# Mixer, latent stores and embedding projection: other engines and queues, one more buffer each

## The chip, the cores and the metric

One Trainium2 chip, one core of it. The metric is the device time of one execution of the whole program, in microseconds (us). The program is one inference step of one layer; all inputs and weights lie in the chip's memory at the start, and the outputs lie there at the end.

## What is computed

1024 prompt rows and 8 x 16 sample rows of width 2048 are treated as one set of 1152 tokens. The reference, cut to what matters here:

```python
xn = rms_norm(x, norm_g)
u, g_pool, c_q, c_kv, k_r, g_mla = split(xn @ w_in)            # 1024, 1024, 512, 256, 64, 1024 columns
pool_out = multiscale_pool(pool_hist, u, pos0, w_pool, pool_scale) * silu(g_pool)
new_pool = concatenate([pool_hist, u], axis=1)[:, -15:]
q, k, v  = ...                                                 # from c_q, c_kv and the caches
mla_out  = chunk_causal_attention(q, k, v) * silu(g_mla)
h = x + concatenate([pool_out, mla_out], axis=-1) @ w_out
y = h + sigmoid(rms_norm(h, ple_norm_g) @ w_ple_gate + b_ple_gate) * (p @ w_ple)

def multiscale_pool(...):      # 4 groups of 256 channels, windows 2, 4, 8, 16
    d = mean of the last w rows of u - u                       # over 15 rows of history and the row itself
    return (d @ w_pool[group]) * pool_scale
```

`p` is a 256-wide input per token; `p @ w_ple` is the embedding projection. For the samples the 15 rows of history come from the input `state_pool`, for the prompt they are zero.

## The kernel before

Everything is held transposed: 128 channels on the partitions, tokens along the row, in three blocks of 384 tokens (`TB`); block 2 is the last 256 prompt tokens and the 128 sample tokens. An f32 product is made as three matmuls over operands split in a high and a low part: ScalarE writes the high part (L68), VectorE (in some places GpSimd) the difference (L69), and `mm3` issues the three matmuls (L77 to L79).

The stages, by the time of the trace: sums of `x` and of the first weights (to about 150 us); the input projection `x @ w_in` in two halves of its inner dimension, "chunk 0" (to 400) and "chunk 1" (to 803); latents to keys and queries, with block 0 of the embedding projection beside (to 980); the first half of its block 1, alone (to 1000); the samples' attention, with the rest of block 1 inside (to 1250); embedding block 2 (to 1285); the prompt's attention and the output projection with its gate (to the end).

**The projection** saves multiplications by taking weights in sums and differences. `Quick.sums` (L150) loads two raw weights `r0`, `r1` (tile `wraw`, three buffers), writes the sums `w12` into a tile `wt` (one buffer, called `a` in the code) and the sums `w34` over `r0`, and splits each into `wh`, `wl`. In chunk 1 the result of each product is added to the partial result of chunk 0, loaded as `q` (L512, three buffers), and handed to `finish` (L521). It scales block 2 if need be, takes SiLU for gates, and stores the result `o` (three buffers) to a scratch tensor by L535: `u` and `gp` (mixer input and its gate), `gm` (attention's gate), `cq`, `ckv`. These 90 stores are on SyncE's queue (SP in the profile), in between the loads of `q` and of the weights.

**The mixer** (`Pool`) runs over chunk 1's products from about 505 to 760 us, on TensorE's spare bank `aux`. For group `g` and token block `t`, `fetch` loads 128 channels of `u` back from scratch (L704; with 15 columns of history of the block before, L703), `gates` loads the two gate tiles into `ev` (L710), `tile` forms the window sums by doubling on VectorE (`window`, L689) and the difference `d` (L693), `split` splits `d` into `dh`, `dl`, and `mix` multiplies by the group's weights `pwh`, `pwl` into `aux`, scales by the gate on VectorE (L749) and stores `mixp` (L750). Loads of `u` and gates are on GpSimd's queue (POOL). In block 2 `tile` also stores the new history (L727), loads the samples' history `us` (L729, one buffer, SP's queue), copies the samples' tokens behind it (L730), sums it, and stores the samples' new history (L732).

**The embedding** (`Embed.block`) takes for each of 16 column tiles a weight `wraw` (L786, ScalarE's queue), splits it, multiplies into `p` (two banks) or `k` (a bank lent by the attention), copies the result to `ev` (two buffers, VectorE, L794) and stores it to the scratch `ple` (L795, ScalarE's queue).

**Order.** The code is written in one order and a scheduler, which lays all instructions on a simulated time line, decides the order on each engine. Each engine then runs its own list strictly in that order, and so does each queue: a DMA whose data are not ready holds all that stand behind it on its engine. Tiles come from rings: a tile's next user waits until all readers of the one that many allocations back are done.

Of the kernel before, what the change touches and what calls it, by code (L numbers as in the profile page):

```python
# [8 lines left out]
AF = mybir.ActivationFunctionType  # L9
ALU = mybir.AluOpType  # L10
# [6 lines left out]
NB = 8  # L17
NS = 16
NTOK = SEQ + NB * NS
P = 128  # L20
KT = D // P
TB = 384
# [108 lines left out]
class Quick:  # L131
# [19 lines left out]
    def sums(self, src, c, rest):  # L151

        k, nc = self.k, self.k.nc
        sub = nc.vector.tensor_tensor
        r0, r1 = [self.raw(s, c) for s in src]
        w0 = self.hl(r0)
        a = k.t(self.tp, [P, 8, P], "wt")
        sub(a[:, :4], r1[:, :4], r0[:, :4], ALU.subtract)
        sub(a[:, 4:], r1[:, 4:], a[:, :4], ALU.subtract)
        w12 = self.hl(a)  # L160
        sub(r0[:, :4], r1[:, 4:], r1[:, :4], ALU.subtract)
        sub(r0[:, 4:], r0[:, 4:], a[:, 4:], ALU.subtract)
        w34 = self.hl(r0)
        w1 = self.hl(r1, 0 if rest else 4)
        return {1: (w0, 0), 2: (w0, 4), 5: (w12, 0), 6: (w12, 4), 7: (w34, 0), 4: (w34, 4), 3: (w1, 4),
                "rest": ((w0, 0), (w1, 0))}
# [86 lines left out]
def phase1(k, sc):  # L253
# [268 lines left out]
    def finish(i, t, ps, q):  # L522
        kind, n = kinds[i] if i < KR else ("kr", 0)
        o = o_tile()
        if q is not None:
            nc.vector.tensor_tensor(o[:], ps, q[:], ALU.add)
            ps = o[:]
        if t == 2:
            nc.vector.tensor_tensor(o[:], ps, R2[:], ALU.mult)
        if kind == "kr":  # L530
            k.later(rope_key(k, lp, aux_bank, o, kc, ks, t, sc))
            return
        if kind in ("gp", "gm"):
            nc.scalar.activation(o[:], o[:], AF.Silu)
        nc.sync.dma_start(sc[kind][t][:, n, :], o[:])  # L535
        if kind not in ("ckv", "cq"):
            return
        if (kind, t) not in acc:
            acc[kind, t] = [k.t(lp, [P, TB], f"acc{t}"), 2 if kind == "ckv" else 4]
            nc.scalar.activation(acc[kind, t][0][:], o[:], AF.Square)  # L540
        else:
            sq = k.t(lp, [P, TB], "sq")
            nc.scalar.activation(sq[:], o[:], AF.Square)
            nc.vector.tensor_tensor(acc[kind, t][0][:], acc[kind, t][0][:], sq[:], ALU.add)
        acc[kind, t][1] -= 1
        if not acc[kind, t][1]:
            k.later(latent_factor(kind, t, acc[kind, t][0]))
# [114 lines left out]
class Pool:  # L662


    def __init__(self, k, pp, aux_bank, inv, sc, wp):
        self.k, self.pp, self.aux, self.inv, self.sc = k, pp, aux_bank, inv, sc
        self.wp, self.hl, self.d = wp, [None, None], [None, None]
        self.u, self.gate = {}, {}

    def weights(self, g):  # L670
        k, pp = self.k, self.pp
# [24 lines left out]
    def fetch(self, ct, t):  # L696

        k, nc, src = self.k, self.k.nc, self.sc["u"]
        u = self.u[ct, t] = k.t(self.pp, [P, HIST + TB], "u", bufs=2)
        if t == 0:  # L700
            nc.vector.memset(u[:, :HIST], 0.0)
        else:
            nc.gpsimd.dma_start(u[:, :HIST], src[t - 1][:, ct, TB - HIST:])  # L703
        nc.gpsimd.dma_start(u[:, HIST:], src[t][:, ct, :])  # L704

    def gates(self, g, t):
        k = self.k
        for n in (2 * g, 2 * g + 1):
            self.gate[n, t] = k.t(self.pp, [P, TB], "ev", bufs=2)
            k.nc.gpsimd.dma_start(self.gate[n, t][:], self.sc["gp"][t][:, n, :])  # L710

    def tile(self, ct, t):
        k, pp, nc, io = self.k, self.pp, self.k.nc, self.k.io
        g, c2 = divmod(ct, 2)
        w = 2 << g
        d = self.d[c2] = k.t(pp, [P, TB], f"d{c2}")
        n = TB if t < NT - 1 else SEQ - TB * (NT - 1)
        u = self.u.pop((ct, t))
        s = self.window(u[:, :HIST + n], n, d[:, :n], w)
        if t == 0:  # L720

            m = w - 1
            x = k.t(pp, [P, 16], "head")
            nc.vector.tensor_tensor(x[:, :m], s[:, HIST:HIST + m], self.inv[:, :m], ALU.mult)
            nc.vector.tensor_tensor(d[:, :m], x[:, :m], u[:, HIST:HIST + m], ALU.subtract)
        if t == NT - 1:
            nc.sync.dma_start(io["npool"][ct][:, 0, :], u[:, n:n + HIST])  # L727
            us = k.t(pp, [P, NB, HIST + NS], "us")
            nc.sync.dma_start(us[:, :, :HIST], io["state_pool"][ct])  # L729
            nc.vector.tensor_copy(us[:, :, HIST:], u[:, HIST + n:].rearrange("p (b s) -> p b s", b=NB))  # L730
            self.window(us[:], NS, d[:, n:].rearrange("p (b s) -> p b s", b=NB), w, (NB,))
            nc.sync.dma_start(io["npool"][ct][:, 1:, :], us[:, :, NS:])  # L732

    def split(self):
        for c, d in enumerate(self.d):
# [3 lines left out]
    def mix(self, g, t):  # L739
        k, pp, nc, sc = self.k, self.pp, self.k.nc, self.sc  # L740
        hl = self.hl
        for o in range(2):
            n = 2 * g + o
            gate = self.gate.pop((n, t))
            ps = self.aux()
            sl = slice(o * P, (o + 1) * P)
            for c in range(2):
                k.mm3(ps[:, :TB], self.wh[:, c, sl], self.wl[:, c, sl], hl[c][0][:], hl[c][1][:], c == 0, c == 1)
            nc.vector.scalar_tensor_tensor(gate[:], ps[:, :TB], k.pool_scale[:, n:n + 1], gate[:], ALU.mult, ALU.mult)  # L749
            nc.sync.dma_start(sc["mixp"][t][:, n, :], gate[:])  # L750


def consts(k):
# [11 lines left out]
class Embed:  # L765
# [8 lines left out]
    def block(self, t, cts=range(KT), bank=None):  # L774
        k, nc, io, pl = self.k, self.k.nc, self.k.io, self.pl
        if t != self.at:
            self.at = t
            self.ph = k.t(pl, [P, 2, TB], "h", F32R)
            self.pl_ = k.t(pl, [P, 2, TB], "l", F32R)
            for c in range(2):  # L780
                raw = k.t(pl, [P, TB], "raw")
                nc.scalar.dma_start(raw[:], io["pT"][t][:, c, :])
                k.split(self.ph[:, c, :], self.pl_[:, c, :], raw[:])
        for ct in cts:
            raw = k.t(pl, [P, 2, P], "wraw", bufs=4)
            nc.scalar.dma_start(raw[:], io["w_ple"][ct])  # L786
            wh = k.t(pl, [P, 2, P], "wh", F32R, bufs=self.bufs)
            wl = k.t(pl, [P, 2, P], "wl", F32R, bufs=self.bufs)
            k.split(wh[:], wl[:], raw[:])
            ps = bank() if bank and ct % 3 else k.t(self.pp, [P, 512], "p", bufs=self.banks)  # L790
            for c in range(2):
                k.mm3(ps[:, :TB], wh[:, c, :], wl[:, c, :], self.ph[:, c, :], self.pl_[:, c, :], c == 0, c == 1)
            ev = k.t(pl, [P, TB], "ev", bufs=2)
            nc.vector.tensor_copy(ev[:], ps[:, :TB])  # L794
            nc.scalar.dma_start(self.sc["ple"][t][:, ct, :], ev[:])  # L795


class Shared:
# [881 lines left out]
```

## Time and profile before

| | |
|---|---|
| runs | 2310.47, 2302.0, 2307.72 us; median 2307.72 us |
| profiled execution | 2295.69 us, of which span 2293.9 us; mean granted TensorE clock 0.983 |
| VectorE, ScalarE, GpSimd busy | 1450.2 us (63%), 985.4 us (43%), 345.7 us (15%) |
| SyncE's queue and ScalarE's queue | 304.18 MB in 234240 packets, 23.21 MB in 19296 packets |
| GpSimd's queue | 9.56 MB in 3584 packets |

The page gives busy times of one execution over its span. `PE` is TensorE, `DVE` VectorE, `ACT` ScalarE, `POOL` GpSimd, `SP` SyncE, which only issues DMAs; "SPq" marks a DMA issue on that queue. A row of the list of waits reads "engine, tile and line that waited <- engine, tile and line (or DMA) waited for: us in all, times, longest". A row of the timeline is start, duration, engine, line, operation, out<-in, shape, and in brackets the idle time ahead of it with what ended it. The clock is the one granted to TensorE: 0.50 means that the matmuls were fed at half speed.

### The profile page before, as it was taken

To read this page: it belongs to the slowest core of one execution; us is meant where nothing else is said; L and a number is where in the kernel's file an instruction comes from. 1 tells how busy PE (TensorE), PEld (TensorE's weight loads), DVE (VectorE), ACT (ScalarE), POOL (GpSimd) and SP (SyncE) were. 2 spreads that over 40 slices of the span, in tenths; PEclk is the share of its full clock that TensorE was granted. 3 is DMA by queue.
4 is the path that set the end of the run, shared out by engine and by line. 5 is a ranking of instruction groups with operands and counts; after the bars stand their busy time and mean duration, and the time that the engine had idled before them with its cause. 6 is when DMAs were issued, how large, how long until landed. Compare 5 with 4: busy or idle time off the path is not lost.

```text
span 2293.9 us, 35989 instructions
## 1 busy us (share of the span) xinstructions
PE 2217.6 (97%) x12856; PEld 2160.4 (94%) x12856; DVE 1450.2 (63%) x3056; ACT 985.4 (43%) x2181; POOL 345.7 (15%) x317
## 2 busy tenths in 40 slices
PE   8989999999899999989999899999999999999999
PEld 7989999999899989979998799999999999999998
DVE  6787777776777668868887765555553345344343
ACT  6533335443333466756665543343342233232222
POOL 0000000001111000033552532221002221111110
PEclk9999999999999999999999799999999999999999
DMA  9574336556666766482222844443263333223221
GB/s 297 185 245 156 126 122 217 166 164 178 184 186 186 220 201 189 122 252 95 92 71 73 246 152 153 129 154 124 82 198 112 101 120 110 86 92 98 85 87 64
DMA packets 257299, 339.24 MB, mean 148 GB/s; under 512 B 45024, under 2 KB 207200, under 8 KB 257120
## 3 DMA queue, kind: packets, MB, share of 16 engines
q1 hardware_dynamic: 234240, 304.18, 42.9%
q10 hardware_dynamic: 19296, 23.21, 3.1%
q0 software_dynamic: 3584, 9.56, 1.7%
q8 instruction: 101, 1.65, 0.3%
q14 instruction: 78, 0.64, 0.1%
HBM read 235.74 MB, written 101.12 MB: 147 GB/s over the span
## 4 chain that ended last, share of the span: by engine, by line
PE 54%; DMA 7%; DVE 6%; issue 2%; ACT 2%; POOL 1%; SPq 0%; ACTq 0%; DVEq 0%; POOLq 0%
PE mm L77 8%; PE mm L79 8%; PE mm L78 8%; PE f L77 3%; PE f L79 3%; PE f L78 3%; PE k L78 2%; PE k L79 2%; PE k L77 2%; PE t L1213 1%; DMA rawcq<-cq 1%; PE o L79 1%; PE o L78 1%; PE s L78 1%; PE s L79 1%
## 5 line engine op out<-in xcount | busy, mean ns | idle before, releaser
L68 ACT ACTIVATE wh<-wraw 128x1024 fp32r<-128x1024 f32 (+3 forms) x237 | 182.2, 770 | 212.9 <-PE mm L177 125.7
L69 DVE TENSOR_TENSOR wl<-wraw,wh 128x1024 fp32r<-128x1024 f32 (+3 forms) x235 | 210.6, 897 | 69.9 <-ACT wh L68 67.3
L1536 DVE TENSOR_TENSOR ev<-mm,R 128x384 f32<-128x384 f32 x48 | 26.7, 557 | 174.2 <-PE mm L79 170.3
L1537 ACT ACTIVATE ev<-ev,gains 128x384 f32<-128x384 f32 x48 | 29.4, 612 | 224.5 <-DVE ev L1536 124.5
L71 ACT ACTIVATE wh<-wraw,gains 128x128 fp32r<-128x128 f32 x256 | 82.0, 391 | 52.5 <-ACT wh L71 31.6
L704 POOL DMA_DIRECT2D u<-u x24 | 13.1, 544 | 602.1 <-DVE frs3a L88 509.3
L1214 ACT ACTIVATE pth<-t 128x512 fp32r<-128x512 f32 (+2 forms) x96 | 46.3, 486 | 131.8 <-PE t L1213 130.8
L72 DVE SCALAR_TENSOR_TENSOR wl<-wraw,gains,wh 128x128 fp32r<-128x128 f32 x256 | 88.0, 390 | 17.5 <-ACT wh L71 16.4
L77 PE MATMUL k<-wkh,ch 128*128 128x448 f32 x256 | 95.2, 373 | 2.1 <-ACT ch L68 1.3
L78 PE MATMUL k<-wkh,cl 128*128 128x448 f32 x256 | 93.6, 365 | 0.6 <-DVE cl L69 0.6
L79 PE MATMUL k<-wkl,ch 128*128 128x448 f32 x256 | 93.7, 366 | 0.0
L79 PE MATMUL mm<-A2l,wh 128*128 128x384 f32 x256 | 86.0, 336 | 0.0
L77 PE MATMUL mm<-A2h,wh 128*128 128x384 f32 x256 | 86.0, 336 | 0.0
L78 PE MATMUL mm<-A2h,wl 128*128 128x384 f32 x256 | 86.0, 336 | 0.0
L77 PE MATMUL mm<-A0h,wh 128*128 128x384 f32 x256 | 85.8, 335 | 0.0
L79 PE MATMUL mm<-A0l,wh 128*128 128x384 f32 x256 | 85.7, 335 | 0.0
L78 PE MATMUL mm<-A1h,wl 128*128 128x384 f32 x256 | 85.7, 335 | 0.0
L78 PE MATMUL mm<-A0h,wl 128*128 128x384 f32 x256 | 85.7, 335 | 0.0
L79 PE MATMUL mm<-A1l,wh 128*128 128x384 f32 x256 | 85.5, 334 | 0.0
L77 PE MATMUL mm<-A1h,wh 128*128 128x384 f32 x256 | 85.5, 334 | 0.0
L1498 DVE TENSOR_TENSOR ev<-mm,ev 128x384 f32<-128x384 f32 x48 | 26.8, 558 | 86.3 <-PE mm L79 85.9
L1342 ACT ACTIVATE sq<-k 128x896 f32<-128x896 f32 x64 | 58.5, 914 | 51.7 <-PE k L1339 50.0
(803 smaller groups left out, 7822.6 us busy)
## 6 DMA issues: line engine op xcount, KB each, us to landing
wraw<-w_in SPq DMA_DIRECT2D x89, 512.0 KB, 4.6
part<-o SPq DMA_DIRECT2D x93, 192.0 KB, 2.7
q<-part SPq DMA_DIRECT2D x93, 192.0 KB, 3.4
wraw<-w_out SPq DMA_DIRECT2D x64, 256.0 KB, 3.4
wraw<-w_ple_gate SPq DMA_DIRECT2D x64, 256.0 KB, 3.2
ple<-ev ACTq DMA_DIRECT2D x48, 192.0 KB, 3.0
fev<-xT SPq DMA_DIRECT2D x48, 192.0 KB, 2.4
hp<-fev SPq DMA_DIRECT2D x48, 192.0 KB, 1.9
```

Source lines behind the costliest of these rows:

```text
L68: nc.scalar.activation(hi, src, AF.Copy)
L69: eng.tensor_tensor(lo, src, hi, ALU.subtract)
L71: nc.scalar.activation(hi, src, AF.Copy, scale=scale)
L72: eng.scalar_tensor_tensor(lo, src, scale, hi, ALU.mult, ALU.subtract)
L77: mm(out, sh, mh, start=start, stop=False)
L78: mm(out, sl, mh, start=False, stop=False)
L79: self.last = mm(out, sh, ml, start=False, stop=stop)
L1214: nc.scalar.activation(pth[:, :n, qq], tp[:, :n, :], AF.Copy)
L1342: nc.scalar.activation(sq[:].rearrange("p (g c) -> p g c", g=2), ps[:, :2, :KW], AF.Square)
L1498: nc.vector.tensor_tensor(h[:], ps[:, :TB], h[:], ALU.add)
L1536: nc.vector.tensor_tensor(g[:], ps[:, :TB], R[t][:], ALU.mult)
L1537: nc.scalar.activation(g[:], g[:], AF.Sigmoid, bias=k.b_ple_gate[:, ct:ct + 1])
```

## The change

Four things: the last weight sums are written into `wt` (`a`) and not over `r0`; the stores of `finish`, of `mixp` and of the new history go from SP's queue to GpSimd's; the mixer's loads of `u` and gates go the other way, and the samples' history is loaded in `fetch`, together with its `u`, into two buffers; the embedding's results are copied by ScalarE into three buffers (which the raw input shares) and stored by GpSimd's queue.

```diff
--- before.py
+++ after.py
@@ -158,9 +158,9 @@
         sub(a[:, :4], r1[:, :4], r0[:, :4], ALU.subtract)
         sub(a[:, 4:], r1[:, 4:], a[:, :4], ALU.subtract)
         w12 = self.hl(a)
-        sub(r0[:, :4], r1[:, 4:], r1[:, :4], ALU.subtract)
-        sub(r0[:, 4:], r0[:, 4:], a[:, 4:], ALU.subtract)
-        w34 = self.hl(r0)
+        sub(a[:, :4], r1[:, 4:], r1[:, :4], ALU.subtract)
+        sub(a[:, 4:], r0[:, 4:], a[:, 4:], ALU.subtract)
+        w34 = self.hl(a)
         w1 = self.hl(r1, 0 if rest else 4)
         return {1: (w0, 0), 2: (w0, 4), 5: (w12, 0), 6: (w12, 4), 7: (w34, 0), 4: (w34, 4), 3: (w1, 4),
                 "rest": ((w0, 0), (w1, 0))}
@@ -532,7 +532,7 @@
             return
         if kind in ("gp", "gm"):
             nc.scalar.activation(o[:], o[:], AF.Silu)
-        nc.sync.dma_start(sc[kind][t][:, n, :], o[:])
+        nc.gpsimd.dma_start(sc[kind][t][:, n, :], o[:])
         if kind not in ("ckv", "cq"):
             return
         if (kind, t) not in acc:
@@ -665,7 +665,7 @@
     def __init__(self, k, pp, aux_bank, inv, sc, wp):
         self.k, self.pp, self.aux, self.inv, self.sc = k, pp, aux_bank, inv, sc
         self.wp, self.hl, self.d = wp, [None, None], [None, None]
-        self.u, self.gate = {}, {}
+        self.u, self.gate, self.us = {}, {}, {}
 
     def weights(self, g):
         k, pp = self.k, self.pp
@@ -700,14 +700,17 @@
         if t == 0:
             nc.vector.memset(u[:, :HIST], 0.0)
         else:
-            nc.gpsimd.dma_start(u[:, :HIST], src[t - 1][:, ct, TB - HIST:])
-        nc.gpsimd.dma_start(u[:, HIST:], src[t][:, ct, :])
+            nc.sync.dma_start(u[:, :HIST], src[t - 1][:, ct, TB - HIST:])
+        nc.sync.dma_start(u[:, HIST:], src[t][:, ct, :])
+        if t == NT - 1:
+            us = self.us[ct] = k.t(self.pp, [P, NB, HIST + NS], "us", bufs=2)
+            nc.sync.dma_start(us[:, :, :HIST], self.k.io["state_pool"][ct])
 
     def gates(self, g, t):
         k = self.k
         for n in (2 * g, 2 * g + 1):
             self.gate[n, t] = k.t(self.pp, [P, TB], "ev", bufs=2)
-            k.nc.gpsimd.dma_start(self.gate[n, t][:], self.sc["gp"][t][:, n, :])
+            k.nc.sync.dma_start(self.gate[n, t][:], self.sc["gp"][t][:, n, :])
 
     def tile(self, ct, t):
         k, pp, nc, io = self.k, self.pp, self.k.nc, self.k.io
@@ -724,12 +727,11 @@
             nc.vector.tensor_tensor(x[:, :m], s[:, HIST:HIST + m], self.inv[:, :m], ALU.mult)
             nc.vector.tensor_tensor(d[:, :m], x[:, :m], u[:, HIST:HIST + m], ALU.subtract)
         if t == NT - 1:
-            nc.sync.dma_start(io["npool"][ct][:, 0, :], u[:, n:n + HIST])
-            us = k.t(pp, [P, NB, HIST + NS], "us")
-            nc.sync.dma_start(us[:, :, :HIST], io["state_pool"][ct])
+            nc.gpsimd.dma_start(io["npool"][ct][:, 0, :], u[:, n:n + HIST])
+            us = self.us.pop(ct)
             nc.vector.tensor_copy(us[:, :, HIST:], u[:, HIST + n:].rearrange("p (b s) -> p b s", b=NB))
             self.window(us[:], NS, d[:, n:].rearrange("p (b s) -> p b s", b=NB), w, (NB,))
-            nc.sync.dma_start(io["npool"][ct][:, 1:, :], us[:, :, NS:])
+            nc.gpsimd.dma_start(io["npool"][ct][:, 1:, :], us[:, :, NS:])
 
     def split(self):
         for c, d in enumerate(self.d):
@@ -747,7 +749,7 @@
             for c in range(2):
                 k.mm3(ps[:, :TB], self.wh[:, c, sl], self.wl[:, c, sl], hl[c][0][:], hl[c][1][:], c == 0, c == 1)
             nc.vector.scalar_tensor_tensor(gate[:], ps[:, :TB], k.pool_scale[:, n:n + 1], gate[:], ALU.mult, ALU.mult)
-            nc.sync.dma_start(sc["mixp"][t][:, n, :], gate[:])
+            nc.gpsimd.dma_start(sc["mixp"][t][:, n, :], gate[:])
 
 
 def consts(k):
@@ -778,7 +780,7 @@
             self.ph = k.t(pl, [P, 2, TB], "h", F32R)
             self.pl_ = k.t(pl, [P, 2, TB], "l", F32R)
             for c in range(2):
-                raw = k.t(pl, [P, TB], "raw")
+                raw = k.t(pl, [P, TB], "ev", bufs=3)
                 nc.scalar.dma_start(raw[:], io["pT"][t][:, c, :])
                 k.split(self.ph[:, c, :], self.pl_[:, c, :], raw[:])
         for ct in cts:
@@ -790,9 +792,9 @@
             ps = bank() if bank and ct % 3 else k.t(self.pp, [P, 512], "p", bufs=self.banks)
             for c in range(2):
                 k.mm3(ps[:, :TB], wh[:, c, :], wl[:, c, :], self.ph[:, c, :], self.pl_[:, c, :], c == 0, c == 1)
-            ev = k.t(pl, [P, TB], "ev", bufs=2)
-            nc.vector.tensor_copy(ev[:], ps[:, :TB])
-            nc.scalar.dma_start(self.sc["ple"][t][:, ct, :], ev[:])
+            ev = k.t(pl, [P, TB], "ev", bufs=3)
+            nc.scalar.activation(ev[:], ps[:, :TB], AF.Copy)
+            nc.gpsimd.dma_start(self.sc["ple"][t][:, ct, :], ev[:])
 
 
 class Shared:
```

Below are rows of the order in which the scheduler puts the instructions (line, operation, out<-in, shape, and the semaphores waited for: "DMASW" is one of a DMA on GpSimd's queue, "DMAHW" one of a DMA on another queue). Names carry a running number; `u_25_84`, `u_26_85`, `u_27_86` are the scratch tensors of mixer input for blocks 0, 1, 2, `part_..` the partial results of chunk 0.

SP's list, where the mixer's first group starts (about 510 to 545 us in the trace of before). Before:

```order
L729 DMA us_5734<-state_pool 128x8x15 [waits DMAHW3_49,PE_49]
L535 DMA u_27_86<-o_5326 128x384 [waits DMAHW4_49,DVE_49]
L512 DMA q_5627<-part_28_87 128x384 [waits DMAHW5_49,Activation_49]
L512 DMA q_5657<-part_29_88 128x384 [waits DMAHW6_49,DMAHW5_49,DVE_49]
L535 DMA u_26_85<-o_5408 128x384 [waits DMAHW7_49,DVE_49]
L512 DMA q_5660<-part_28_87 128x384 [waits DMAHW0_49,Activation_49]
L673 DMA wraw_5484<-w_pool 128x512 [waits DMAHW1_49,DVE_49]
L535 DMA u_25_84<-o_5423 128x384 [waits DMAHW2_49,DVE_49]
L512 DMA q_5677<-part_29_88 128x384 [waits DMAHW6_49,DMAHW3_49,Activation_49]
L512 DMA q_5754<-part_30_89 128x384 [waits DMAHW4_49,DVE_49]
L535 DMA gp_7_66<-o_5468 128x384 [waits Activation_49]
L143 DMA wraw_5630<-w_in 128x1024 [waits DMAHW1_49,DVE_49]
```

The same place of the changed kernel:

```order
L707 DMA us_5591<-state_pool 128x8x15
L707 DMA us_5731<-state_pool 128x8x15 [waits DMAHW5_49]
L512 DMA q_5659<-part_29_88 128x384 [waits DMAHW7_49,DVE_49]
L703 DMA u_5494<-u_25_84 128x15 [waits DMAHW1_49,DVE_49]
L512 DMA q_5662<-part_28_87 128x384 [waits DMAHW0_49,Activation_49]
L673 DMA wraw_5484<-w_pool 128x512 [waits DVE_49]
L704 DMA u_5494<-u_26_85 128x384 [waits DMAHW2_49,DMASW4_49]
L512 DMA q_5679<-part_29_88 128x384 [waits DMAHW6_49,DMAHW3_49,Activation_49]
L512 DMA q_5754<-part_30_89 128x384 [waits DMAHW4_49,DVE_49]
L143 DMA wraw_5632<-w_in 128x1024 [waits DMAHW5_49,DMAHW1_49,DVE_49]
L704 DMA u_5435<-u_25_84 128x384 [waits DMASW5_49]
L143 DMA wraw_5634<-w_in 128x1024 [waits DMAHW7_49,DVE_49]
```

The stores that waited for `o` have left the list, two loads of the samples' history stand at its head, and in place of the stores stand loads of `u`, which wait for a store on GpSimd's queue to land; loads of `q` and of weights stand behind them.

VectorE's list where the first group's block 2 ends (about 550 to 560 us). Before:

```order
L689 TENSOR_TENSOR s_1140_5737<-us_5734 128x8x30 [waits DMAHW3_49,DVE_49]
L701 MEMSET u_6004 128x15 [waits DMAHW3_49]
L159 TENSOR_TENSOR wt_5638<-wraw_5632,wt_5638 128x512 [waits DVE_49]
L693 SCALAR_TENSOR_TENSOR d_1137_5729<-s_1140_5737,us_5734 128x128 [waits DVE_49]
L689 TENSOR_TENSOR s_1142_5742<-u_5726 128x270 [waits DMASW3_49,DMASW2_49,DVE_49]
L730 COPY us_5746<-u_5726 128x8x16 [waits DMAHW6_49]
L693 SCALAR_TENSOR_TENSOR d_1141_5741<-s_1142_5742,u_5726 128x256 [waits DVE_49]
L210 TENSOR_TENSOR u_1133_5692<-mm_5656,s_1130_5674 128x384 [waits PE_49,Activation_49]
L701 MEMSET u_6007 128x15 [waits DMAHW0_49,DVE_49]
L689 TENSOR_TENSOR s_1144_5749<-us_5746 128x8x30 [waits DMAHW1_49]
```

The same place of the changed kernel:

```order
L689 TENSOR_TENSOR s_1141_5739<-us_5591 128x8x30 [waits DMAHW4_49,DVE_49]
L701 MEMSET u_6004 128x15 [waits DMASW1_49]
L732 COPY us_5731<-u_5728 128x8x16 [waits DMAHW6_49]
L693 SCALAR_TENSOR_TENSOR d_1139_5733<-s_1141_5739,us_5591 128x128 [waits DVE_49]
L689 TENSOR_TENSOR s_1143_5744<-u_5728 128x270 [waits DMAHW5_49,DVE_49]
L693 SCALAR_TENSOR_TENSOR d_1142_5743<-s_1143_5744,u_5728 128x256 [waits DVE_49]
L210 TENSOR_TENSOR u_1134_5694<-mm_5658,s_1131_5676 128x384 [waits PE_49,Activation_49]
L689 TENSOR_TENSOR s_1144_5749<-us_5731 128x8x30 [waits DVE_49]
```

The second channel tile's sum over the samples' history (last row) waited for a DMA and now waits for VectorE's own work alone; its history tile `us_5731` was loaded with its `u`.

GpSimd's list behind the samples' attention (about 1245 to 1285 us), where the splits of the first prompt tiles stand. Before:

```order
L69 TENSOR_TENSOR ql_13555<-raw_13552,qh_13554 128x512 [waits DMAHW0_49,Activation_49]
L69 TENSOR_TENSOR kl_13561<-raw_13558,kh_13560 128x512 [waits DMAHW2_49,Activation_49]
L1164 TENSOR_TENSOR stk_13567<-raw_13564,stk_13567 64x512 [waits DMAHW6_49,Activation_49,Pool_49]
L69 TENSOR_TENSOR vl_13573<-raw_13570,vh_13572 128x512 [waits DMAHW0_49,Activation_49,Pool_49]
L69 TENSOR_TENSOR krl_13551<-raw_13576,krh_13550 128x384 [waits DMAHW2_49,PE_49,Activation_49]
```

The same place of the changed kernel (`ple_24_83` is block 2 of the scratch tensor):

```order
L797 DMA ple_24_83<-ev_13728 128x384 [waits DMASW5_49,Activation_49]
L69 TENSOR_TENSOR ql_13555<-raw_13552,qh_13554 128x512 [waits DMAHW5_49,Activation_49]
L69 TENSOR_TENSOR kl_13561<-raw_13558,kh_13560 128x512 [waits DMAHW6_49,Activation_49]
L797 DMA ple_24_83<-ev_13744 128x384 [waits DMASW6_49,Activation_49]
L797 DMA ple_24_83<-ev_13760 128x384 [waits DMASW7_49,Activation_49]
L1166 TENSOR_TENSOR stk_13567<-raw_13564,stk_13567 64x512 [waits DMAHW1_49,Activation_49,Pool_49]
L69 TENSOR_TENSOR vl_13573<-raw_13570,vh_13572 128x512 [waits DMAHW3_49,Activation_49,Pool_49]
```

The embedding's stores now stand among the splits, and one that stands behind a split starts after it.

## The prediction

> **What bounds the kernel now.** First the page's busy times, with the clock granted to TensorE in 40 slices:
>
> ```profile
> PE 2217.6 (97%) x12856; PEld 2160.4 (94%) x12856; DVE 1450.2 (63%) x3056; ACT 985.4 (43%) x2181; POOL 345.7 (15%) x317
> PEclk9999999999999999999999799999999999999999
> ```
>
> TensorE is busy for 97% of the span. The change removes no matmul, so it can only win time in which TensorE waits for an engine or transfer that it touches, and what a lower clock adds to such a wait. So the list of TensorE's waits comes next; of it, the rows of the mixer (`aux`) and of the embedding (`p`):
>
> ```profile
> PE aux L77 <- DVE ev L749: 9.0, 2, 4.6
> PE aux L77 <- ACT dh L68: 3.5, 3, 2.0
> PE aux L79 <- DVE dl L69: 2.6, 1, 2.6
> PE p L77 <- DVE ev L794: 3.6, 5, 1.8
> ```
>
> The timeline of TensorE gives the places of the four longest in the mixer, and the windows behind them the clock (columns: us, busy time of PE, PEld, DVE, ACT and POOL with counts, clock, DMA share, GB/s); the last window lies between two of these places:
>
> ```profile
> 565.51 0.66 PE L77 MATMUL aux<-dh,pwh 128*128 128x384 f32 x1 [4.42 <-DVE ev L749]
> 627.27 0.66 PE L77 MATMUL aux<-dh,pwh 128*128 128x384 f32 x1 [4.56 <-DVE ev L749]
> 691.09 0.67 PE L77 MATMUL aux<-dh,pwh 128*128 128x384 f32 x1 [2.03 <-ACT dh L68]
> 695.33 1.01 PE L79 MATMUL aux<-dl,pwh 128*128 128x384 f32 x2 [2.60 <-DVE dl L69]
> ...
> 564.86:571.68 6.82, 6.17 (x19) 6.20 (x20) 3.57 (x6) 0.45 (x2) 1.00 (x2) 0.50 0.72 247
> 626.30:633.12 6.82, 5.84 (x18) 5.88 (x19) 3.89 (x7) 0.59 (x2) 1.60 (x3) 0.50 0.80 241
> 691.15:701.39 10.24, 7.63 (x23) 7.13 (x24) 6.87 (x14) 2.24 (x4) 2.08 (x4) 0.50 0.58 162
> 571.68:626.30 54.62, 49.78 (x282) 49.14 (x281) 36.80 (x73) 18.10 (x30) 7.56 (x15) 1.00 0.66 175
> ```
>
> After each stop the clock is 0.50, so half of the busy time there is lost too: 6.17/2 = 3.1, 5.84/2 = 2.9 and 7.63/2 = 3.8 us. The three places cost 4.42 + 3.1 = 7.5, 4.56 + 2.9 = 7.5 and 2.03 + 2.60 + 3.8 = 8.4, together **23.4 us**. That is nearly the whole prize.
>
> What is late there? VectorE's waits between 500 and 760 us, and three rows of its timeline:
>
> ```profile
> DVE wt L158 <- DMA wraw<-w_in: 15.8, 7, 4.4
> DVE s L689 <- DMA us<-state_pool: 9.0, 3, 4.1
> DVE us L730 <- DMA npool<-us: 4.0, 2, 2.5
> DVE u L234 <- DMA q<-part: 3.1, 3, 1.4
> ...
> 557.66 0.41 DVE L689 TENSOR_TENSOR s<-us 128x240 f32<-128x240 f32 x1 [4.07 <-DMA us<-state_pool]
> 621.27 0.41 DVE L689 TENSOR_TENSOR s<-us 128x240 f32<-128x240 f32 x1 [1.25 <-DMA us<-state_pool]
> 694.23 0.57 DVE L689 TENSOR_TENSOR s<-u 128x398 f32<-128x398 f32 x1 [3.83 <-DMA u<-u]
> ```
>
> Eight us ahead of the first stop VectorE stands 4.07 us for the samples' history, whose load the single buffer holds back until the previous one's store has landed. Before the second it stands 2.5 us for that buffer and 1.25 us for the load. The third has another tail, the chain that ended last:
>
> ```profile
> 682.26 8.19 DMA u<-o
> 691.09 3.04 DMA u<-u
> ```
>
> A store of `u` took 8.19 us, and its load back 3.04.
>
> **The change, part by part**, against the profiled execution's 2295.69 us.
>
> *History loaded with its input, two buffers.* Both loads stand at the head of SP's list, and the second sum waits for no DMA any more. At the first place 4.07 us of VectorE's lateness go against a stop of 4.42; at the second 2.5 + 1.25 = 3.8 against 4.56. What is left, 0.4 and 0.8 us, is one or two of VectorE's instructions (0.41 and 0.57 us in the rows above). Next late on VectorE are the weights' sums, with 15.8 us of waits for `wraw`, which the earlier release of `r0` should shorten. I take both stops with their low clock as gone: -15.0. Bounds: 0, if VectorE then waits for `wraw` instead, and -15.0.
>
> [...]
>
> *Loads of `u` and gates to SP, stores to POOL.* At the third place the history load goes too, but the chain runs over the store and load of `u`, which stay. The store leaves a queue in which it stood between other loads, for one that carries little:
>
> ```profile
> L704 POOL DMA_DIRECT2D u<-u x24: 536/538/686, 509.8 to 734.8; - x24
>   DMA u<-o: 72.7, 9
> L535 SPq DMA_DIRECT2D u<-o x24: 319/328/803, 505.2 to 709.7; - x24
> SPq L535 <- ACT o L534: 54.7, 22, 6.7
> u<-o SPq DMA_DIRECT2D x24, 192.0 KB, 3.1
> u<-u POOLq DMA_DIRECT2D x24, 192.0 KB, 4.0
> ```
>
> An issue takes 538 ns on POOL against 328 ns on SP (first and third row), and 192 KB land in 4.0 against 3.1 us, as loads; how a store lands from POOL's queue no row shows. I take the loads' 4.0, between the bounds 3.1 and the 8.19 us above. So a single store lands 0.2 + 0.9 = 1.1 us later, but no longer waits behind loads for other outputs. Of the 8.4 us I count half, -4.2, between 0 and -8.4.
>
> The new wait: SP now waits for the landing before it loads `u`, as POOL did for 72.7 us in 9 waits (second row), 8.1 us each; `q` and weights stand behind. Against that, 54.7 us of SP's own waits for `o` (fourth row) go over to POOL. The cover is the ring of `q` (first row; columns of the second: duration min/median/max in ns, first and last start):
>
> ```profile
> q<-part SPq DMA_DIRECT2D x86, 192.0 KB, 3.4
> L732 SPq DMA_DIRECT2D npool<-us x8: 389/465/612, 544.7 to 748.1; - x8
> ```
>
> 86 loads in the 415 us of this view (400 to 815) make one each 4.8 us; with two loaded ahead a hold is hidden up to 9.7 us. A hold of 8.1 plus the load's 3.4 exceeds it by 1.8 us. Bounds: 0 and 9 x 1.8 = 16 us. VectorE's waits above have 3 for `q` among 86, the longest 1.4 us, so `q` is seldom late; I charge two of nine: **+3.6**.
>
> Of the other stores that move, none is waited for nearby: the gates' and latents' are read a group or a stage later. `npool<-us`, in 1024 short pieces, takes 389 to 612 ns to issue on SP (second row); on POOL somewhere between 0.54 us and eight times that (a load of `u`, 128 pieces, takes 538 ns there), so up to 8 x 3.8 = 30 us of POOL's time over the mixer. POOL's 7.56 us in the 54.62 of the window above cover that: 0, and for the range what a late store of `u` costs, the same 16 us as above.
>
> *Weights' sums over `wt`.* No instruction more. `w34` must wait until the split of `w12` has read `wt`, and `r0` comes free one split sooner. VectorE has both ends inside its 15.8 us of waits for `wraw`; TensorE's list has no wait for these sums in chunks 0 and 1. 0, with +-2 us for the start, where VectorE is fullest.
>
> *Embedding.* The copies, VectorE's and a like one on ScalarE, and the stage's window:
>
> ```profile
> L794 DVE COPY ev<-p 128x384 f32<-128x384 f32 x38 | 21.0, 551 | 12.1 <-PE p L79 7.7 <-DMA ple<-ev 4.3
> L295 ACT ACTIVATE o<-mm 128x384 f32<-128x384 f32 x47 | 22.6, 480 | 29.2 <-issue 13.5 <-PE mm L177 9.1 <-PE mm L438 6.3
> 980.00:1005.00 25.00, 18.03 (x99) 15.07 (x98) 18.10 (x48) 12.16 (x30) 0.44 (x1) 1.00 0.82 247
> ```
>
> Each of 48 copies goes from 551 ns on the fuller engine (18.10 of 25 us) to 480 ns on the emptier (12.16). TensorE's 3.6 us of waits for `ev` come mostly from here, and I count 3.0 of them as gone, between +1 (ScalarE also makes the high parts that these matmuls need) and -3.6. Where block 2 ends, the chain runs over three stores, and on POOL stand long splits:
>
> ```profile
> 1250.91 3.20 DMA ple<-ev
> 1255.80 4.62 DMA ple<-ev
> 1271.68 4.28 DMA ple<-ev
> L69 POOL TENSOR_TENSOR ql<-raw,qh 128x512 fp32r<-128x512 f32 x16 | 21.5, 1346 | 28.7 <-ACT qh L68 28.7
> ```
>
> With two buffers a copy waits for the store two back; with three there is one more copy's time. At most the 12.1 us of the chain go. But loads of the attention's first tiles lie beside them, and a store that stands behind a split starts up to 1.35 us later. I take -4, a third, between +1.35 x 2 = +2.7 and -12.1.
>
> Sum: -15.0 - 4.2 + 3.6 - 3.0 - 4.0 = **-22.6**, so 2273.1 for an execution like the profiled one. The runs' median, 2307.72, stands at 1.0052 of it; scaled so, **2285 us**.
>
> **Rivals.** *The new wait gives it back.* All nine holds reach TensorE: +16 in place of +3.6 brings the sum to about -10; if the restarts behind some of them come at half clock (as after the 2.03 us stop) another 4, so -6: **2302**. For it speaks the order: loads of `u` stand ahead of `q` and weights. Against it, that SP waited for `o` just as long.
>
> *Slower.* One mechanism: the stores of `u` land later from POOL's queue, and the holds outgrow the ring. Landing 7 to 8 us, like the 8.19 above, makes a hold 8.1 + 8.19 - 3.1 = 13.2, and 13.2 + 3.4 - 9.7 = 6.9 us of each of nine holds reach TensorE: 62 us less the 26 of gains without the charge, +36: **2344**. It decides against the gain from (26 + 11.5)/9 = 4.2 us per hold, a hold of 10.5 us. Against it: loads on that queue land in 4.0 us in the middle.
>
> *More goes.* The third place falls wholly (-8.4), no new wait, and the chain at the tail loses its 12.1: -15.0 - 8.4 - 3.6 - 12.1 = -39: **2268**.
>
> *VectorE holds up POOL's issues.* POOL issues 178 stores in place of 64 loads. If each store of `u` waited for one instruction of VectorE (0.6 us), 24 x 0.6 = 14 us would be laid on the holds, and the sum would be -9: **2299**. Against it: with VectorE busy for 36.80 of 54.62 us, the 24 loads' issues took 536 to 686 ns, none longer. [...]
>
> *It doesn't do what it says:* the history loaded ahead might still wait. The order rules that out for the second tile of a group, so it has no chance of its own.
>
> **How the numbers follow.** Forecast 0.55, more 0.12, given back 0.22, VectorE's hold 0.03, slower 0.08. 0.5% of the median is 11.5 us, about what a measurement of this kernel can tell: faster is below 2296.2, slower above 2319.2. Faster 0.55 + 0.12 = 0.67, same 0.22 + 0.03 = 0.25, slower 0.08. The range runs from 2266, just under the "more" case, to 2310, which takes in the given-back case with the +-2 of the sums and the +2.7 of the tail; outside are the slower case and tails of the others.
>
> **What would show it.** Right: no stop at `aux` over 2 us at the first two places, clock 1.00 from 560 to 690 us; VectorE without waits for `us` or `npool`; SP's waits for `u<-o` below 9.7 us, and no more waits for `q` than now; no `ple<-ev` in the chain near 1250 to 1285. Wrong: stops at `aux` for `wraw` sums or for `u`; landings of `u<-o` from POOL over 6 us; issues on POOL over 0.7 us; `PE p` waiting for ScalarE.

## The result and the profile after

| | median, us | runs | ratio to before, 95% interval |
|---|---|---|---|
| before | 2306.59 | 4, 2302.0 to 2310.47 | |
| changed | 2292.09 | 4, 2291.72 to 2293.2 | 0.9941 [0.9927, 0.9955] |

The change makes the kernel 0.59% faster, [0.45%, 0.73%]; 13.6 us of 2306.59. Forecast were 2285 us with a range of 2266 to 2310, and -22.6 us on the way there. Sign and range held and the size was 0.6 of what was forecast. As the experiments show, the mixer gave about half of what the forecast had for it and the embedding more, so that the total lies nearer than its parts.

The page of the changed kernel, its busy times and clock:

```profile
PE 2211.1 (97%) x12856; PEld 2154.0 (94%) x12856; DVE 1439.5 (63%) x3008; ACT 1004.0 (44%) x2229; POOL 410.8 (18%) x431
PEclk9999999999999999999999899999999999999999
```

VectorE lost the 48 copies and ScalarE took them; GpSimd is 65 us busier with issues. TensorE's waits in the mixer, 540 to 780 us of the changed kernel (us in all, times, longest):

```profile
PE aux L77 <- ACT dh L68: 9.6, 4, 3.7
PE mm L175 <- DVE u L221: 6.4, 1, 6.4
PE aux L79 <- DVE dl L69: 1.1, 1, 1.1
PE aux L77 <- DVE ev L751: 0.7, 1, 0.7
```

The waits of `aux` for `ev`, 9.0 us in the trace of before, are 0.7. But waits for `dh` rose from 3.5 to 9.6, and there is a stop of 6.4 us at a main product, which the mixer's rows of before don't have. In all there are 17.8 us, where the trace of before had 15.1. The chain that ended last shows where the new stop comes from (start, us, what):

```profile
733.73 13.74 DMA ev<-gp
...
747.59 0.17 DVE ev L751
...
748.13 0.56 DVE u L221
748.73 0.69 PE mm L175
```

A load of a gate, 192 KB, took 13.74 us, against 3.8 in the middle of all 24. VectorE waited for it, and the product's operand `u` was next in VectorE's list. The DMA view of 728 to 750 us shows that everything was late there (busy tenths in 40 slices, GB/s; then the issues: count, KB each, median us to landing):

```profile
DMA  2014757788997939799899799999795999976106
GB/s 109 0 30 53 272 165 284 187 274 261 208 176 67 56 39 87 70 159 226 168 204 186 209 320 336 361 267 197 57 71 82 132 212 206 228 281 281 75 22 59
...
wraw<-w_in SPq DMA_DIRECT2D x2, 512.0 KB, 10.7
q<-part SPq DMA_DIRECT2D x4, 192.0 KB, 7.8
...
ev<-gp SPq DMA_DIRECT2D x3, 192.0 KB, 7.6
npool<-us POOLq DMA_DIRECT2D x2, 60.0 KB, 9.9
npool<-u POOLq DMA_DIRECT2D x2, 7.5 KB, 6.6
```

In three of the slices the DMA engines are nine tenths busy while only 56 to 87 GB/s move. In this stretch are two stores of the samples' history, `npool<-us`: 60 KB each, but in 1024 pieces of 60 bytes, because the tile holds the new rows with gaps between them. They were issued at 730.97 and 735.14 us and landed after 8.0 and 11.9 us, so both were in flight together. That they hold up the transfers beside them became theory C of the experiments.

### The profile page after: what moved, and what is told of

Same layout as the page of the kernel before. It is cut to its first block, busy times and chain, and to the rows that moved or that the text cites. A ratio compares the mean times of both kernels' runs of the same rounds, so it can differ in the third digit from the quotient of the medians.

```text
span 2290.6 us, 36006 instructions
## 1 busy us (share of the span) xinstructions
PE 2211.1 (97%) x12856; PEld 2154.0 (94%) x12856; DVE 1439.5 (63%) x3008; ACT 1004.0 (44%) x2229; POOL 410.8 (18%) x431
## 4 chain that ended last, share of the span: by engine, by line
PE 66%; DMA 12%; DVE 9%; issue 8%; ACT 3%; POOL 2%; SPq 0%; ACTq 0%; DVEq 0%; POOLq 0%
PE mm L78 8%; PE mm L77 8%; PE mm L79 8%; PE mm L175 5%; PE mm L176 5%; PE mm L177 5%; PE f L77 3%; PE f L79 3%; PE f L78 3%; PE k L79 2%; PE k L78 2%; PE k L77 2%; DMA u<-u 1%; PE t L1215 1%; PE pb L77 1%
## 5 line engine op out<-in xcount | busy, mean ns | idle before, releaser
L68 ACT ACTIVATE wh<-wraw 128x1024 fp32r<-128x1024 f32 (+3 forms) x207 | 150.2, 729 | 146.3 <-PE mm L177 83.8
L69 DVE TENSOR_TENSOR wl<-wraw,wh 128x512 fp32r<-128x512 f32 (+3 forms) x205 | 172.0, 842 | 66.7 <-ACT wh L68 58.8
L1539 ACT ACTIVATE ev<-ev,gains 128x384 f32<-128x384 f32 x48 | 29.4, 612 | 224.2 <-DVE ev L1538 124.4
L68 ACT ACTIVATE wh<-wt 128x1024 fp32r<-128x1024 f32 x60 | 63.4, 1056 | 74.0 <-PE mm L177 48.5
L69 DVE TENSOR_TENSOR wl<-wt,wh 128x1024 fp32r<-128x1024 f32 x60 | 73.3, 1221 | 24.8 <-ACT wh L68 24.6
L1510 POOL TENSOR_TENSOR R<-R,sq 128x384 f32<-128x384 f32 x45 | 46.0, 1023 | 210.3 <-ACT sq L1509 210.3
```

Source lines behind the costliest of these rows:

```text
L68: nc.scalar.activation(hi, src, AF.Copy)
L69: eng.tensor_tensor(lo, src, hi, ALU.subtract)
L1510: nc.gpsimd.tensor_tensor(acc[t][:], acc[t][:], sq[:], ALU.add)
```

## Experiments

Each was timed beside runs of the kernel before on its chip. The change's four things make three parts: the sums, the mixer part (its second and third) and the embedding part. Ratios are to the kernel before.

| run | what | ratio, 95% interval |
|---|---|---|
| e1 | before, once more | 0.9991 [0.9976, 1.0006] |
| e2 | mixer part alone | 0.9979 [0.9965, 0.9994] |
| e3 | embedding part alone | 0.9952 [0.9935, 0.9969] |
| e4 | sums alone | 0.9996 [0.9979, 1.0013] |
| e5 | embedding: only eviction by ScalarE | 0.9995 [0.9978, 1.0013] |
| e6 | embedding: only store on GpSimd's queue | 1.0001 [0.9990, 1.0013] |
| e9 | embedding: only three buffers | 1.0004 [0.9986, 1.0021] |
| e10 | embedding: eviction and buffers | 0.9986 [0.9969, 1.0003] |
| e12 | mixer part and sums | 0.9966 [0.9952, 0.9980] |
| e7 | changed kernel, history in whole pieces | 0.9831 [0.9809, 0.9853] |
| e8 | changed kernel, no history store | 0.9836 [0.9814, 0.9858] |
| e11 | before, history in whole pieces | 0.9901 [0.9871, 0.9932] |

**e1, the same program again.** No edit.

> The kernel before, unchanged, for a second profile: the profiled execution of before took 2295.69 us while its timed runs took 2302 to 2310. Theory A (the trace of before is one of several courses that the same program takes): the ratio is 1.000 within 0.2%, and the new profile has other stops of TensorE than the first, in sum up to 11 us more. Rival B (the first profile is typical and the rest lies outside the span): the same stops at the same places, within 1 us each.

Measured: 2298.78 to 2311.75 us in ten runs; the profiled one took 2307.87 us. Its waits of TensorE from 540 to 780 us:

```profile
PE aux L77 <- ACT dh L68: 13.4, 5, 5.9
PE aux L77 <- DVE ev L749: 5.0, 1, 5.0
PE aux L79 <- DVE dl L69: 3.8, 1, 3.8
```

That is 22.2 us, 7.1 more than in the first trace, with longer stops at the same four places and two waits more. Theory A holds: the same program takes more than one course, and the trace on which the prediction stood was the lighter of the two. Below, stops are compared with this second trace, and times by their ratios alone.

**e2, e4 and e12: mixer and sums.** e2 takes from the change (e4 is the first hunk of the diff alone, e12 both together):

```diff
-        nc.sync.dma_start(sc[kind][t][:, n, :], o[:])
+        nc.gpsimd.dma_start(sc[kind][t][:, n, :], o[:])
...
-        nc.gpsimd.dma_start(u[:, HIST:], src[t][:, ct, :])
+        nc.sync.dma_start(u[:, HIST:], src[t][:, ct, :])
+        if t == NT - 1:
+            us = self.us[ct] = k.t(self.pp, [P, NB, HIST + NS], "us", bufs=2)
+            nc.sync.dma_start(us[:, :, :HIST], self.k.io["state_pool"][ct])
...
-            nc.sync.dma_start(sc["mixp"][t][:, n, :], gate[:])
+            nc.gpsimd.dma_start(sc["mixp"][t][:, n, :], gate[:])
```

> Only the mixer's part of the change: stores of finish, mixp and npool on GpSimd's queue, loads of u, gates and samples' history on SP's, history loaded with its input in two buffers; sums and embedding as before. Theory A (the gain is the mixer's): 2294 to 2297 us, ratio 0.994 to 0.996, the stop of 4.42 us at 565 us gone, and the new stop of 6.43 us near 749 us there as in the changed kernel. Rival B (the mixer's gain is eaten by that new stop, and the embedding brings the gain): ratio 0.998 to 1.001.

> Only the weights' last sums written over wt instead of the raw weight. Theory A: within 0.1% of before, as charged with 0 +-2 us in the prediction. Rival C (the sums' buffer release is what the mixer needed: VectorE waited 15.8 us for raw weights): ratio 0.996 to 0.998, and these waits fall to under 5 us.

> The changed kernel with the embedding as before. Theory H (mixer's part and sums pay only together, since without the sums VectorE waits 19.6 us for raw weights): ratio 0.994 to 0.997, no stop over 3 us at 566 us. Rival I (mixer's part -0.21% and sums -0.04% add, the rest of the change's 0.59% is the embedding's): ratio 0.997 to 0.999.

Measured: the mixer part alone gave 0.21%, next to rival B's band and far from theory A's, and the new stop of 6.43 us is 0.9 us there; the sums alone gave nothing that can be told from none, though VectorE's waits for raw weights fell to 1.7 us; both together gave 0.34%. The first two stops are still there with the mixer part alone, by TensorE's timeline:

```profile
566.79 0.66 PE L77 MATMUL aux<-dh,pwh 128*128 128x384 f32 x1 [4.68 <-DVE ev L751]
628.05 0.66 PE L77 MATMUL aux<-dh,pwh 128*128 128x384 f32 x1 [5.63 <-DVE ev L751]
```

VectorE no longer waits for the history. In its place it waits, in that kernel from 500 to 770 us, for raw weights and for `q`; below them the longest from its timeline:

```profile
DVE wt L158 <- DMA wraw<-w_in: 19.6, 8, 6.3
DVE u L234 <- DMA q<-part: 16.7, 3, 7.2
...
560.24 0.56 DVE L234 TENSOR_TENSOR u<-u,q 128x384 f32<-128x384 f32 x1 [7.23 <-DMA q<-part]
```

One late transfer has taken the place of another, six us ahead of the same stop. It is the same at the second place, where VectorE waits 7.19 us for `q` until 621.90. Both of these loads of `q` stood on SP's list behind a gate's load, which waited 8.1 us until a store of `mixp`, now on GpSimd's queue, had landed and so freed its buffer; then they took 8.0 and 6.7 us to land, beside a store of the history. With the sums too (e12) the wait for raw weights is gone, the stops are 13.9 us, and the one at 566 us is down to 1.1 (now at 564.14), but others remain:

```profile
PE aux L77 <- ACT dh L68: 6.7, 3, 5.4
PE mm L175 <- DVE u L221: 5.2, 1, 5.2
PE aux L79 <- DVE dl L69: 2.0, 1, 2.0
```

The longest, 5.36 us, belongs to the second place, so that one the change did not remove; the stop at the main product is there without the embedding's part. e12 meets theory H's expectation, though the intervals of e2 and e12 overlap, so that the sums help the mixer part is likely and not shown by times; the traces show by which wait.

**e3, e5, e6, e9 and e10: the embedding.** Three edits, alone and together (where there are three buffers, the raw input shares them, as in the change):

```diff
-            ev = k.t(pl, [P, TB], "ev", bufs=2)
-            nc.vector.tensor_copy(ev[:], ps[:, :TB])
-            nc.scalar.dma_start(self.sc["ple"][t][:, ct, :], ev[:])
+            ev = k.t(pl, [P, TB], "ev", bufs=3)                      # e9, e10, e3
+            nc.scalar.activation(ev[:], ps[:, :TB], AF.Copy)         # e5, e10, e3
+            nc.gpsimd.dma_start(self.sc["ple"][t][:, ct, :], ev[:])  # e6, e3
```

> Only the embedding's part: evictions by ScalarE into three buffers, stores on GpSimd's queue. Theory A (mixer brings the gain): ratio 0.998 to 1.000, that is 0 to 4 us. Rival B (embedding brings it): ratio 0.994 to 0.996, 9 to 14 us less, and no ple store in the chain between 1250 and 1285 us.

> Of the embedding's part only the eviction by ScalarE; two buffers, raw input in a tile of its own, store on ScalarE's queue as before. Theory A (VectorE's load in the embedding was the limit, the eviction is what wins): most of the embedding's gain of 0.48%, ratio 0.995 to 0.997, and TensorE's waits for wl between 1250 and 1285 us shorter. Rival B (the waits for ple stores, that is buffers or queue): ratio 0.998 to 1.001.

> Of the embedding's part only the store on GpSimd's queue; VectorE evicts into two buffers. Theory A (eviction): ratio 0.999 to 1.001. Rival B (48 stores of 0.33 us, and the waits of their queue for the eviction, stood between ScalarE's loads and splits): ratio 0.995 to 0.998.

> Of the embedding's part only the three buffers, shared with the raw input; VectorE evicts, ScalarE's queue stores. Eviction alone (e5) and store alone (e6) gave nothing, all three together 0.48%. Theory E (the wait of an eviction for the store two back was the limit): ratio 0.995 to 0.997. Rival F (the parts need each other: an eviction on ScalarE pays only when ScalarE's list does not also wait for stores and buffers): 0.998 to 1.001.

> Eviction by ScalarE and three buffers, stores left on ScalarE's queue. Theory E: as e9, 0.995 to 0.997. Rival F: between, 0.996 to 0.999; if it gives the whole 0.48%, the store's queue does not matter.

Measured: all three edits give 0.48%, none alone gives anything, eviction and buffers 0.14% with an interval that holds zero. So theory E falls, and rival F's bands hold: the parts need each other. The store's queue together with only one of the other two was not run, so whether all three are needed is not shown. The trace of e9 shows what buffers alone change. In e1 VectorE waits for stores of `ple` from 1240 to 1315 us:

```profile
DVE ev L794 <- DMA ple<-ev: 5.9, 5, 2.3
```

In e9 no engine waits for such a store; TensorE's longest waits there, from 975 to 1315 us, are others, of which the second was 1.7 us in e1 and the others under 0.8:

```profile
PE s L77 <- ACT e L1198: 5.3, 2, 4.0
PE aux L1368 <- DVE mx L1366: 4.5, 4, 1.9
PE p L77 <- ACT wh L68: 4.4, 1, 4.4
```

TensorE's waits for `ev` are 3.4 us in both, so the buffers did not reach it, and ScalarE is late with the high parts `wh` and the exponentials `e`; why was not traced.

What the three together bring looks less like a matter of waits than of the clock. From 800 to 1330 us TensorE's stops sum to 31.3 us in e1 and 29.4 in e3, but the stretches at a clock of 0.50 sum to 37.5 us in e1 and 20.5 in e3. At half speed the difference of 17.0 is worth 8.5 us of the 11.1. In e5, e6, e9 and e10 these stretches sum to 37.5 to 51.2 us. This is one trace of each; the changed kernel has 30.7 us, and the kernels with the embedding as before have 30.7 (e4) to 44.4 (e2, e12). So it is a likely account and not a shown one.

**e7, e8 and e11: the history's pieces.** e7, on the changed kernel; e8 leaves out the last store alone, and with it that output; e11 makes the same edit in the kernel before, with one `hs` buffer, loaded in the old place on SP's queue:

```diff
-            us = self.us[ct] = k.t(self.pp, [P, NB, HIST + NS], "us", bufs=2)
-            nc.sync.dma_start(us[:, :, :HIST], self.k.io["state_pool"][ct])
+            hs = self.us[ct] = k.t(self.pp, [P, NB, HIST], "hs", bufs=2)
+            nc.sync.dma_start(hs[:], self.k.io["state_pool"][ct])
...
-            us = self.us.pop(ct)
+            us = k.t(pp, [P, NB, HIST + NS], "us")
+            hs = self.us.pop(ct)
+            nc.scalar.activation(us[:, :, :HIST], hs[:], AF.Copy)
...
-            nc.gpsimd.dma_start(io["npool"][ct][:, 1:, :], us[:, :, NS:])
+            nc.scalar.activation(hs[:], us[:, :, NS:], AF.Copy)
+            nc.gpsimd.dma_start(io["npool"][ct][:, 1:, :], hs[:])
```

> The changed kernel, with the samples' history loaded into and stored from a tile without gaps, so that each partition's 480 bytes are one piece instead of eight of 60; two small ScalarE copies for each of 8 channel tiles are added. Theory C (the 1024-piece stores hold up every transfer behind them: landings of 7 to 14 us beside them, stop of 6.43 us near 749 us): landings of all transfers in the mixer at about 3 us, the 749 us stop gone, 8 to 20 us less than the changed kernel, ratio 0.986 to 0.991. Rival D (the transfers are late because of sheer volume, some 3 MB in 20 us): ratio 0.993 to 0.996, as the changed kernel.

> The changed kernel without the 8 stores of the samples' new history (that output is left out; the loads of 60-byte pieces stay). Theory C: landings beside it fall to 3 to 4 us, ratio 0.987 to 0.992. Rival D: ratio 0.993 to 0.996. If e7 gains and this one does not, the loads of the pieces are what holds the transfers up.

> The kernel before, with only the samples' history loaded into and stored from a tile without gaps (one buffer, SP's queue, loaded in the place of before, two ScalarE copies for each of 8 tiles). Theory C in its strong form (the 60-byte pieces alone are the mixer's delay, whatever the order): ratio 0.988 to 0.992, the stops of 4.4 to 6 us at aux under 2 us. Rival G (the change's order is needed as well, e7's 1.69% is the two together): ratio 0.993 to 0.997, stops for the raw weights stay.

Measured: e7 takes 2264.64 us and is the fastest kernel of the study. It is 1.7% faster than before; by the two ratios, 0.9831/0.9941 = 0.989, it is 1.1% faster than the changed kernel. The history's bytes are the same, each partition's 480 now in one piece; the landings are not. The changed kernel's issues with their landings, 400 to 815 us:

```profile
q<-part SPq DMA_DIRECT2D x86, 192.0 KB, 3.1
...
ev<-gp SPq DMA_DIRECT2D x24, 192.0 KB, 3.8
...
us<-state_pool SPq DMA_DIRECT2D x8, 60.0 KB, 5.7
npool<-us POOLq DMA_DIRECT2D x8, 60.0 KB, 8.3
```

and e7 in the same view:

```profile
q<-part SPq DMA_DIRECT2D x86, 192.0 KB, 2.9
...
ev<-gp SPq DMA_DIRECT2D x24, 192.0 KB, 3.3
...
hs<-state_pool SPq DMA_DIRECT2D x8, 60.0 KB, 3.2
npool<-hs POOLq DMA_DIRECT2D x8, 60.0 KB, 3.4
```

Medians of all neighbours hardly move, since only those beside the 8 stores are late. Taken apart, they show it: of the 192 KB transfers issued from 500 to 780 us, those that overlap such a store took 7.6 us in the middle in the changed kernel (43 of them, at most 13.7), and 3.2 where they overlap neither it nor a load of the history. In the kernel before the two numbers are 5.2 (at most 8.8) and 3.3, in e7 3.6 and 3.1. In e7 TensorE has no wait in the list from 540 to 780 us. Two windows show it for e1, the changed kernel and e7 in turn (us, busy PE with its count of matmuls, PEld, DVE, ACT, POOL, clock, DMA share, GB/s):

```profile
540.00:690.00 150.00, 136.29 (x748) 135.04 (x747) 102.78 (x200) 47.32 (x79) 20.99 (x40) 0.95 0.67 176
690.00:780.00 90.00, 81.55 (x449) 80.35 (x448) 65.67 (x125) 32.63 (x55) 9.57 (x18) 0.94 0.71 189
```

```profile
540.00:690.00 150.00, 141.80 (x791) 140.39 (x789) 106.74 (x212) 48.95 (x81) 33.46 (x59) 0.98 0.69 182
690.00:780.00 90.00, 80.30 (x435) 79.34 (x436) 65.36 (x122) 32.83 (x56) 17.43 (x31) 0.94 0.66 193
```

```profile
540.00:690.00 150.00, 150.00 (x861) 150.00 (x860) 119.07 (x234) 56.60 (x102) 34.42 (x64) 1.00 0.66 208
690.00:780.00 90.00, 89.65 (x516) 89.33 (x514) 69.15 (x129) 41.32 (x70) 17.73 (x33) 1.00 0.69 221
```

In the first window these are 748, 791 and 861 matmuls, in the second 449, 435 and 516: what the change gains up to 690 us it partly loses again behind it, where the late gate stands, and e7 loses nothing in either. e8 gives the same as e7 within the intervals, so the store does the harm and the loads of 60-byte pieces little; rival D (sheer volume) falls, since e7 moves the same bytes.

The time of e11 lies in theory C's band: whole pieces alone bring 0.99% to the kernel before. Its stops at `aux` sum to 8.4 us, but the longest is 3.9, where theory C asked for under 2, and VectorE still waits 15.2 us for raw weights, as rival G had it. The change on top of whole pieces is worth 0.9831/0.9901 = 0.993, about 0.7% (0.3% to 1.1% by the two intervals), near its 0.59% without them. The embedding's part alone brings 0.48%, and no run has whole pieces with the mixer's part alone; so whether the mixer's new order is worth anything beside whole pieces stays open.

## Why the prediction was right and wrong

*What bounds.* Right: the time was to be had only where TensorE waits. Weak: one trace was taken for the kernel. A second of the same program had 22.2 us of stops in the mixer, not 15.1.

*"I take both stops with their low clock as gone: -15.0."* This step failed. It read VectorE's wait for the history, 4.07 us ahead of a stop of 4.42, as its cause. The wait went, and with the mixer part alone the stops stayed at 4.68 and 5.63, each behind a wait of 7.2 us for `q` (e2). The bound of 0 that the step itself gave, "if VectorE then waits for `wraw` instead", is what that run showed, with `q` in the place of `wraw`. In the changed kernel the first stop is gone, by e12 against e2 through the sums' earlier release (one trace of each); the second is 3.74 us, at 625.43, and others of 2.50, 1.88 and 6.43 us came. Mixer and sums brought 0.34%, 7.8 us, [4.6, 11.1], where the sum had -15.6. That remainders of 0.4 and 0.8 us would cost no clock, which the -15.0 takes in, was the author's assumption; no run shows it as a rule. What the changed kernel shows is two cases: a clock of 1.00 in the 5.6 us behind the 0.71 us left at the first place, at 564.73, and of 0.50 behind the 3.74 at the second.

*The new wait, +3.6.* Small, as charged, in the changed kernel, but with a hold left out. SP's waits there, 500 to 770 us:

```profile
SPq L704 <- DMA u<-o: 26.7, 8, 10.1
SPq L713 <- DMA mixp<-ev: 26.0, 15, 9.1
```

The holds for `u` are 3.3 us each and not the 8.1 of the prediction, but SP waits just as long at the gates' loads for stores of `mixp` to land, and that hold the prediction did not count. VectorE's waits for `q` are 4.2 us in the changed kernel, after 3.1 before, so the rival "the new wait gives it back" did not come there. With the mixer part alone they are 16.7 us and reach TensorE: there it came in part.

*"Of the other stores that move, none is waited for nearby", 0.* Here a wait was put at nothing. The issue of `npool<-us` took 901 ns on GpSimd's queue, inside the bounds of 0.54 and 4.3 us. But VectorE waits in the changed kernel for the other history store, `npool<-u`, 7.5 KB, which must land before the tile `u` can be written again; the rows are from 500 to 770 us:

```profile
DVE u L701 <- DMA npool<-u: 6.9, 1, 6.9
DVE wl L69 <- DMA npool<-u: 5.0, 1, 5.0
```

In the trace of before this wait is 1.0 us. The first ends at 559 us, where the wait for the history stood, the second at 621 us (there the write of `u` and that of `wl` start together), four us ahead of the stop of 3.74. These two stores were issued at 549.86 and 612.02 us, about 2.4 and 3.6 us behind the first piece-wise store of their pair, and landed after 9.2 and 8.9 us; the ones ahead of that store landed after 2.3 and 2.4.

*The pieces themselves.* As the price of moving the stores, 0 is not shown to be wrong: whole pieces bring 0.99% to the kernel before and 1.1% to the changed one. What the prediction overlooked is that the pieces hold up the transfers beside them in both kernels, and so what was late behind the history. The change also puts more of them in flight at once: the single buffer of before kept the two stores of each pair apart, and with two buffers all four pairs overlap. The row of before that shows it stands in the same DMA view as the landings that the prediction read (400 to 815 us), and the step left it out:

```profile
npool<-us SPq DMA_DIRECT2D x8, 60.0 KB, 6.5
```

*Sums, 0 +-2.* Right alone (-0.04% [-0.21%, +0.13%]); with the mixer part they do what "the earlier release of `r0` should shorten" says.

*Embedding, -3.0 for the eviction and -4.0 for the buffers.* The sum of 7 lies just outside the measured 11.1 us, [7.2, 15.0], and neither term is what was measured: each edit alone gave nothing (e5, e9), and together with the store's queue they give 11. At the tail, the chain of the changed kernel holds no landing of a `ple` store, as forecast; e9 shows that taking VectorE's waits for them away is by itself worth nothing.

*VectorE holds up POOL's issues.* It did not. Its stores took 538 to 682 ns to issue, the 8 of 60-byte pieces 901 to 904.

*The signs.* That the forecast's total came near is in part luck: too much for the mixer and too little for the embedding. Several of its own signs came out against it in the changed kernel: a stop over 2 us at the second place (3.74), a clock of 0.97 and not 1.00 from 560 to 690 us, VectorE's waits for `npool`, and issues of 901 ns on POOL.

## What to carry to other kernels

Before moving a transfer to another queue, look at its pieces: the row of a small transfer that lands late can be a sign that the transfers beside it land late too (in the kernel before, 60 KB in 6.5 us, and the 192 KB transfers beside it in 5.2, against 3.3 with none of the history's transfers beside them). Two small copies for each tile on an engine with room cured more (0.99%, e11) than the mixer's reordering of queues with the sums (0.34%, e12).

A wait that is as long as the stop behind it need not be its cause. Look for what is late next in the same engine's list, and test with that part alone. And take two traces of a program whose runs spread by 0.6% (2298.78 to 2311.75 us) before trusting its stops to the microsecond.

## What the runs showed of the hardware

A store of 60 KB in 1024 pieces of 60 bytes landed after 8.3 us in the middle and in 128 pieces of 480 bytes after 3.4 (changed kernel and e7); with two of the former in flight, a 192 KB load took 13.74 us on another queue. A 7.5 KB store on the same queue landed after 2.3 us ahead of such a store and after 9.2 us behind it. Moving the stores to GpSimd's queue did not shield the loads on SP's: the load of 13.74 us was on SP's, and the 192 KB transfers that overlap such a store took 7.6 us in the middle in the changed kernel, 5.2 in the kernel before. The 60 KB are the same in both forms; here it was the eight times more, eight times smaller pieces that mattered.

Behind some stops the clock fell late. In the trace of before it was 0.50 from the first matmul after 4.42 us (565.51 to 566.31). After a stop of 3.74 us at 625.43 in the changed kernel, the first matmuls ran at a clock of 1.00 (625.40 to 626.20), and it fell after them (windows as above, 1.6 us each, the last 1.8):

```profile
625.40:627.00 1.60, 1.57 (x7) 1.57 (x8) 1.60 (x3) 0.40 (x1) 0.00 (x0) 0.83 1.00 352
627.00:628.60 1.60, 1.60 (x6) 1.60 (x6) 1.60 (x4) 0.00 (x0) 0.54 (x1) 0.50 1.03 222
628.60:630.20 1.60, 1.60 (x7) 1.60 (x7) 1.60 (x4) 0.00 (x0) 0.00 (x0) 0.60 0.84 252
630.20:632.00 1.80, 1.80 (x13) 1.80 (x12) 1.76 (x5) 0.00 (x0) 0.54 (x1) 1.00 0.88 269
```

It was 0.50 throughout only in the second window and back at 1.00 in the fourth. A stop of 2.50 us, at 601.78, had the same behind it (0.50 from 603.0 to 604.7), and so had one of 1.88 us, at 721.52 (0.50 from 722.03 to 725.44). So these stops, of 1.88 to 3.74 us, each cost a stretch at half rate, as those of 2.03 and 2.60 us at the third place in the prediction did.
